# Five places of a two-layer decoder kernel reordered: the dilated fetch, the last pair result, the first gate, the weight differences and the last square of the final norm

## The chip, the core and the metric

The kernel runs on one core of one Trainium2 chip. The metric is the device time of one execution in microseconds (us), lower is better. Engines are called by the profile's names: PE (matmuls and transposes), PEld (its weight loads), DVE and ACT (elementwise work, ACT also the activation functions), POOL, and SP, which here only issues DMA transfers.

## The reference

The reference is a decoder trunk of two layers over 1024 tokens of width 1024, in 32-bit floating point. Cut to what matters, one layer is:

```
h    = rmsnorm(x, norm1[l]);  proj = h @ w_in[l]        # q, k, v of two mixers, and two gates
o_a  = dilated_mixture(qa, ka, va)                      # 3 groups of 4 heads: (window, dilation) = (128, 1), (512, 4), (2048, 16)
o_b  = stick_breaking_attention(qb, kb, vb)             # 4 heads: beta * product of (1 - beta) over later keys
x    = x + (sigmoid(gates_a) * (o_a @ w_br[:A]) + sigmoid(gates_b) * (o_b @ w_br[A:])) @ w_o[l]
h2   = rmsnorm(x, norm2[l]);  a, v = split(h2 @ w_up[l])
x    = x + (gelu(conv3(a)) * v) @ w_down[l]
```

Behind both layers stands one more `rmsnorm(x, norm_f)`, whose result is the output. A `rmsnorm` divides each token by the root of the mean of its squares over the 1024 features.

## The kernel before

**Products.** All activations lie with features on the partitions and tokens along the rows, in two halves of 512 tokens (`n` = 0 and 1). A 32-bit operand is split into a rounded high part and the rest: `split` (L138) does it with a cast on ACT (L141) and a subtraction on DVE (L148), and a product is then three matmuls, high by high, high by low and low by high (L1014 to L1016). Names ending in `h` or `hi` are high parts, names ending in `l` or `lo` low ones.

**Pairs.** The input projection is made pair by pair: `pair` (L1114) loads two blocks of 128 columns of `w_in` (tile `in_a`, L1128, two transfers of 512 KB) and makes both blocks for both token halves with seven products in place of eight. For that it forms sums and differences of weight quarters on DVE (L1142, L1145, L1148, L1149), splits them (`piece`, tiles `w_hi` and `w_lo`) and adds the products up afterwards. The last of the four results is copied out of the accumulation bank by L1198 (tile `last`) and handed to `put(1, 1, ...)`. For keys and queries of the dilated groups `put` is that of `pair_kq` (L1202 to L1215): it splits the result into high and low part (`in_parts`, L597 on ACT and L598 on DVE; tiles `kq_h` and, in place, `last`) and issues two stores to a scratch tensor `tk` in memory (L1211, SP).

**Attention between the products.** A generator, called `Dense` in the code, hands out the pair products step by step; items of attention work are placed between them, so that PE always has a product to do while ACT and DVE work for attention. `dense.at(k, f)` runs `f` after k more such steps. A stick-breaking item computes scores `z` (L644, L645), two sigmoids on ACT (`beta`, L711; `stay`, L712), a scan along the keys on DVE (L731 for the first stretch of keys, L733 for the others), a multiplication of `beta` by the scanned `stay` on DVE (L738), transposes on PE (`sb_t`, L746), a split into `sbh` and `sbl`, and the product with the values. A near item takes the first of the three dilated groups; its statistics leave by way of `st_r` (L842, L843). A far item takes the two groups of dilation 4 and 16: `fetch_kq` (L866 to L874) loads its keys and queries from `tk` with three transfers (L872: 384 KB; L874: two of 128 KB) into one of two tiles `t_kq`, used in turn, then `score` (L644, L645) reads the tile, and transposed probabilities `t` are split into `p1h` (ACT) and `p1l` (DVE) and multiplied by the values (L931, L933; accumulation tile `o`). `fold` (L659 on ACT, L660 on DVE) brings a finished `o` out. There are 16 far items in each layer; `fetch_v` (L878) loads their values.

**Gates and branches.** When the last pairs run, the stored gates come back (`gin`, L1358) and `gate_on` (L1360 to L1364) applies the sigmoid with two instructions per tile. In front of the first of them ACT loads another table of functions (`ACT_TABLE_LOAD`). At the same time `in_two` splits the stick-breaking output into `oh_b` and `ol_b`.

**The end.** `leave` (L1866) makes the final norm. `norm_add` (L470) squares a block of features (`sq`, ACT, L477) and adds it to `ACC` (`nrm`, DVE, L479). `factor` (L1872) sums `ACC` over the partitions with matmuls against a column of ones (L1877), takes the root (L1878) and the reciprocal (L1879). `turned` (L1881) transposes the result back to token rows (`y_t`, L1884), and `out_part` scales it and stores it (L1891, L1893, L1895).

**What sets the order.** PE runs in the order in which the code was recorded. The order on ACT, DVE, SP and POOL comes from a scheduler that simulates the program and works by priorities; `tc.high_priority(offset=AHEAD)` lifts instructions above others, and `tc.add_manual_dep(a, b, NO_SYNC)` puts instruction `a` somewhere behind `b` in an engine's order, without a semaphore. The dictionary `LAST` holds names of instructions to stand behind: `LAST["act"]` and `LAST["dve"]` are the two halves of the latest split of attention probabilities (`parts`, L647), `LAST["pair"]` the latest pair result. Each engine starts its instructions in its own fixed order, and an instruction that waits for a semaphore holds up those behind it. On SP that holds for the issue of transfers.

In the names below, numbers behind an underscore tell buffers of one name apart; `x2` at the end of a row of an order means two such instructions in a row.

Of the kernel before, what the change touches and what calls it, by code (L numbers as in the profile page):

```python
# [16 lines left out]
P = 128  # L17
# [39 lines left out]
def f32(ap):  # L57
    return ap.bitcast(F32)
# [3 lines left out]
def trunk_kernel(ctx, tc, x, norm1, w_in, b_gate, w_br, w_o, norm2, w_up, conv_w, conv_b, w_down, norm_f, out, depth=None, probe=None):  # L62
# [404 lines left out]

    ACC = [None, None]

    def norm_add(n, e, first=False, sub=slice(0, HF)):  # L470
# [6 lines left out]
        act.activation(sq, xc(n, e, sub), AF.Square)  # L477
        if not first:
            dve.tensor_tensor(acc, acc, sq, ALU.add)  # L479

# [114 lines left out]
    def in_parts(c, scale, hi, lo, x):  # L595
        if c:
            one = act.mul(hi, x, scale)  # L597
            two = dve.scalar_tensor_tensor(lo, x, scale, f32(hi), ALU.mult, ALU.subtract)  # L598
        else:
            one = act.copy(hi, x)  # L600
            two = dve.tensor_tensor(lo, x, f32(hi), ALU.subtract)
        return one.ins.name, two.ins.name

    def kq_half(c, w, n):
        o = bank("ps", "kq_ps"[c:])
        yield from product(o, [(w[k], h_part(n, k)) for k in range(KD)])
        hi, lo = small("kq_h", F32R), small("kq_l", F32R)
        LAST["head"] = in_parts(c, SCALE, hi, lo, o)
        LAST["pair"] = LAST["head"][0]
        keep_kq(c, n, 0, hi, lo)  # L610
        yield
# [82 lines left out]
    def stick_item(dense, u, qp):  # L694
# [29 lines left out]
        def scans(most):  # L724

            while SCANS and most:
                most -= 1
                _, bt, sv, c0, c1, L = SCANS.pop(0)
                rev = sv[:, c0:c1][:, ::-1]
                if c1 == L:  # L730
                    one = dve.tensor_tensor_scan(rev, rev, over[:, HF - (c1 - c0) : HF][:, ::-1], 1.0, ALU.mult, ALU.max)  # L731
                else:
                    one = dve.tensor_tensor_scan(rev, rev, zero[:, 0:1].to_broadcast([P, c1 - c0]), sv[:, c1 : c1 + 1], ALU.mult, ALU.add)  # L733
                if "dve" in LAST:
                    tc.add_manual_dep(one.ins, LAST["dve"], NO_SYNC, reason="in turn")
                k0, k1 = max(0, c0 - 1), c1 - 1
                with tc.high_priority(offset=AHEAD):
                    dve.tensor_tensor(bt[:, k0:k1], bt[:, k0:k1], sv[:, k0 + 1 : k1 + 1], ALU.mult)  # L738

        def turn(kb):  # L740
            while any(x[0] is shared and x[4] > kb * P for x in SCANS):
# [124 lines left out]
    def fetch_kq(i):  # L866

        if i < 2:
            t = R["kq", i] = sb.tile([P, 2, 3, 256], F32R, tag="xa", bufs=4, name="t_kq")
            pool.memset(f32(t[64:128, :, 2, :]), 0.0)  # L870
        t, there = R["kq", i % 2], tk[i // 8][i // 4 % 2, :, i % 4]
        nc.sync.dma_start(f32(t[0:64]), there[:, :, 1:4, :])  # L872
        for g in range(2):
            nc.sync.dma_start(f32(t[64:128, g, 0:2, :]), there[:, g, 0:3:2, :])  # L874

    def fetch_v(i):
        t = R["v", i] = R["slots"][:, i % 4]
# [236 lines left out]
    def pair(dense, l, offs, tiled, put):  # L1114
# [33 lines left out]
        yields(after(dve.tensor_tensor(a21, a22, a11, ALU.subtract)))  # L1148
        yields(after(dve.tensor_tensor(a11, a12, a11, ALU.subtract)))  # L1149
# [52 lines left out]
    def pair_kq(dense, l, g, pr):  # L1202
        off = 256 * g + P * pr

        def put(c, n, x, room=None):
            hi = room.bitcast(F32R) if room is not None else small("kq_h", F32R)
            hv, lv, xv = (t.rearrange("p (r j) -> p r j", r=4) for t in (hi, x.bitcast(F32R), x))
            in_parts(c, -SCALE, hv, lv, xv)
# [66 lines left out]
    def mixer(l, pending):  # L1275
# [84 lines left out]
        def gate_on(i):  # L1360
            if i < len(todo):
                n, e = todo[i]
                for ab in range(2):
                    act.activation(gts[i][:, ab, :], gts[i][:, ab, :], AF.Sigmoid, bias=bg[:, 0, ab * KD + e : ab * KD + e + 1])  # L1364

        def gate_in(i):
            gate_load(i)
# [498 lines left out]
    def leave(rest):  # L1866
# [5 lines left out]
        def factor(n, cs, tag="t"):  # L1872

            tot = bank(tag, "nrm_t")
            a, b = 4 * n + cs[0], 4 * n + cs[-1] + 1
            for c in cs:
                pe.matmul(tot[:, c : c + 1], ACC[n][:, c * P : (c + 1) * P], ones, start=True, stop=True, skip_group_check=True)  # L1877
# [27 lines left out]
        def features():  # L1905
            for e in range(4):
                yield from rest(5, e)
                norm_add(1, 4 + e, e == 0)
                gain_in(1, 4 + e)

        def tokens(sub):
            for e in range(4):
                for _ in rest(6, e, sub):
                    pass
                norm_add(1, e, False, sub)
                gain_in(1, e, sub)
                yield

# [17 lines left out]
        factor(1, (2, 3), "ps")  # L1936
        some += [turned(1, 2, 0, "ps"), turned(1, 3, 0, "s")]
        for t in some:
            out_part(*t)
# [211 lines left out]
```

## Time and profile before

| | |
|---|---|
| time, median of 3 runs | 2620.95 us (2620.76 to 2621.39) |
| time of the profiled execution | 2621.54 us |
| its span in the profile | 2619.8 us |
| granted TensorE clock | 1.000 |
| PE busy | 2606.3 us, 99% of the span |
| DVE busy | 2089.1 us, 80% |
| ACT busy | 1358.8 us, 52% |
| POOL busy | 100.4 us, 4% |
| moved by DMA | 468.22 MB, 179 GB/s |

The profiled execution took 0.59 us more than the median of the runs. Rows of the profile begin with a start time in us from the start of the span; then comes a duration, the engine, the line of the kernel, the operation, output and inputs, and, where the engine was idle before it, how long and what it waited for. Ends of matmuls are modelled: the profile gives a matmul of 512 columns some 0.39 us, while the next one may start 0.23 us after it. Layer 0 runs in about the first half of the span, layer 1 in the second; the same places come again some 1293 us later.

### The profile page before, as it was taken

The page shows a single profiled execution, that of the slowest core. Times are in us where ns is not written, and L with a number is a line of the kernel's source. Part 1 is how long each engine was busy: PE and PEld are TensorE (multiplying, and loading weights), DVE is VectorE, ACT ScalarE, POOL GpSimd, SP SyncE. Part 2 cuts the span into 40 slices and gives each one's busy share as a digit, 9 for nine tenths or more (in the row PEclk, how much of TensorE's full clock was granted, in tenths as well). Part 3 has the DMA queues.
Part 4 walks back from the last instruction along what each step waited for, and adds up shares of the span by engine and source line. Part 5 has one row for each costly group of instructions (what it writes and reads, how often), then busy time and mean ns, then how long its engine had stood idle before and what let it go on. Part 6 is the DMA issues. An engine that isn't in the chain of part 4 may idle for free.

```text
span 2619.8 us, 36195 instructions
## 1 busy us (share of the span) xinstructions
PE 2606.3 (99%) x12732; PEld 2185.4 (83%) x12732; DVE 2089.1 (80%) x3485; ACT 1358.8 (52%) x2533; POOL 100.4 (4%) x135
## 2 busy tenths in 40 slices
PE   9999999999999999999999999999999999999999
PEld 8888888888888888888888888888888888888887
DVE  8877777795988888897677778777869888889965
ACT  6555666574554555422445555666645555544225
POOL 3000000030000000000000000000300000000000
PEclk9999999999999999999999999999999999999999
DMA  7434578873344444688344436787633344446962
GB/s 255 152 117 135 163 202 219 212 245 93 93 145 154 143 169 137 240 325 311 145 150 141 129 124 187 198 224 212 209 97 116 129 156 150 147 167 257 347 240 112
DMA packets 400418, 468.22 MB, mean 179 GB/s; under 512 B 24309, under 2 KB 315501, under 8 KB 398445
## 3 DMA queue, kind: packets, MB, share of 16 engines
q1 hardware_dynamic: 400220, 465.90, 55.1%
q8 instruction: 101, 1.65, 0.3%
q14 instruction: 81, 0.66, 0.1%
q10 hardware_dynamic: 16, 0.00, 0.0%
HBM read 303.23 MB, written 162.59 MB: 178 GB/s over the span
## 4 chain that ended last, share of the span: by engine, by line
PE 94%; DVE 2%; ACT 2%; DMA 1%; issue 1%; SPq 0%; POOL 0%; DVEq 0%; ACTq 0%; POOLq 0%
PE u_a L1014 6%; PE u_a L1016 6%; PE u_a L1015 6%; PE d_ps L1763 5%; PE d_ps L1764 5%; PE d_ps L1765 5%; PE i_a L1014 5%; PE i_a L1016 4%; PE i_a L1015 4%; PE u_c L1014 3%; PE u_c L1016 3%; PE u_c L1015 3%; PE i_c L1014 2%; PE i_c L1016 2%; PE i_c L1015 2%; PE o_ps L182 2%
## 5 line engine op out<-in xcount | busy, mean ns | idle before, releaser
L141 ACT CAST w_hi<-up_a 128x512 fp32r<-128x512 f32 x280 | 174.0, 622 | 277.1 <-DVE up_a L1617 120.6
L148 DVE TENSOR_TENSOR w_lo<-up_a,w_hi 128x512 fp32r<-128x512 f32 x280 | 189.6, 689 | 83.4 <-ACT w_hi L141 83.4
L141 ACT CAST w_hi<-in_a 128x512 fp32r<-128x512 f32 x252 | 156.1, 622 | 163.4 <-PE i_c L1015 38.3
L148 DVE TENSOR_TENSOR w_lo<-in_a,w_hi 128x512 fp32r<-128x512 f32 x252 | 173.0, 688 | 74.9 <-ACT w_hi L141 65.8
L1771 DVE TENSOR_TENSOR x<-x,d_ps 128x512 f32<-128x512 f32 (+1 forms) x228 | 153.8, 676 | 64.9 <-PE d_ps L1765 61.5
L1763 PE MATMUL d_ps<-gd_in,w_hi 128*128 128x512 f32 (+1 forms) x340 | 130.1, 383 | 0.0
L1764 PE MATMUL d_ps<-gd_in,w_hi 128*128 128x512 f32 (+1 forms) x340 | 129.9, 382 | 0.0
L1765 PE MATMUL d_ps<-gd_in,w_lo 128*128 128x512 f32 (+1 forms) x340 | 129.9, 382 | 0.0
L1014 PE MATMUL u_a<-t_hi,w_hi 128*128 128x512 f32 x320 | 124.6, 389 | 0.0
L1016 PE MATMUL u_a<-t_hi,w_lo 128*128 128x512 f32 x320 | 124.6, 389 | 0.0
L1015 PE MATMUL u_a<-t_lo,w_hi 128*128 128x512 f32 x320 | 124.6, 389 | 0.0
L1016 PE MATMUL u_a<-hh,w_lo 128*128 128x512 f32 x320 | 124.6, 389 | 0.0
L1014 PE MATMUL u_a<-hh,w_hi 128*128 128x512 f32 x320 | 124.6, 389 | 0.0
L1015 PE MATMUL u_a<-hl,w_hi 128*128 128x512 f32 x320 | 124.6, 389 | 0.0
L1014 PE MATMUL i_a<-hh,w_hi 128*128 128x512 f32 x288 | 119.2, 414 | 0.0
L1014 PE MATMUL i_a<-t_hi,w_hi 128*128 128x512 f32 x288 | 118.4, 411 | 0.0
L1763 PE MATMUL d_ps<-gd_in,wd 128*128 128x512 f32 (+1 forms) x292 | 114.0, 390 | 0.0
L1016 PE MATMUL i_a<-hh,w_lo 128*128 128x512 f32 x288 | 113.2, 393 | 0.0
L1016 PE MATMUL i_a<-t_hi,w_lo 128*128 128x512 f32 x288 | 113.1, 393 | 0.0
L1015 PE MATMUL i_a<-t_lo,w_hi 128*128 128x512 f32 x288 | 113.0, 392 | 0.0
L1765 PE MATMUL d_ps<-gd_in,wd 128*128 128x512 f32 (+1 forms) x292 | 112.9, 387 | 0.0
L1764 PE MATMUL d_ps<-gd_in,wd 128*128 128x512 f32 (+1 forms) x292 | 112.9, 387 | 0.0
(379 smaller groups left out, 7839.6 us busy)
## 6 DMA issues: line engine op xcount, KB each, us to landing
gd<-g SPq DMA_DIRECT2D x154, 512.0 KB, 3.3
gd_in<-gd SPq DMA_DIRECT2D x154, 512.0 KB, 6.2
up_a<-in_w_up_dram SPq DMA_DIRECT2D x80, 512.0 KB, 5.3
in_a<-in_w_in_dram SPq DMA_DIRECT2D x72, 512.0 KB, 5.4
wd_raw<-in_w_down_dram SPq DMA_DIRECT2D x22, 1024.0 KB, 11.2
gin<-gs SPq DMA_DIRECT2D x32, 512.0 KB, 4.3
w_raw<-in_w_o_dram SPq DMA_DIRECT2D x64, 256.0 KB, 2.9
gs<-u SPq DMA_DIRECT2D x48, 256.0 KB, 4.0
```

The lines of the kernel that those rows point to most:

```text
L141: one = act.copy(hi, src)
L148: two = dve.tensor_tensor(lo, src, f32(hi), ALU.subtract)
L182: pe.matmul(o, lh, rh, start=(first and i == 0), stop=False, skip_group_check=share)
L1014: pe.matmul(o, w[0][:, c], rh, start=(first and i == 0), stop=False, skip_group_check=True)
L1015: pe.matmul(o, w[0][:, c], rl, start=False, stop=False, skip_group_check=True)
L1016: pe.matmul(o, w[1][:, c], rh, start=False, stop=(last and i == 3), skip_group_check=True)
L1763: pe.matmul(o[:, sub], wh[:, c], gh[:, sub], start=(i == 0 and k in (0, 4, 5)), stop=False, skip_group_check=True)
L1764: pe.matmul(o[:, sub], wh[:, c], gl[:, sub], start=False, stop=False, skip_group_check=True)
L1765: pe.matmul(o[:, sub], wl[:, c], gh[:, sub], start=False, stop=(i == m - 1), skip_group_check=True)
L1771: dve.tensor_tensor(x, x, o[:, sub], ALU.add)
```

## The change

There are five edits.

1. Dilated fetch: the three transfers of `fetch_kq` are issued at high priority.
2. Last pair result: for the pairs of dilated keys and queries, the split and the two stores of the last result run two steps later, and the split is put behind the latest split of probabilities on both engines.
3. First gate: the two sigmoids of the first gate tile are put behind the latest cast of probabilities on ACT.
4. Weight differences: the two differences that used to be L1148 and L1149 (now both L1152) are put behind the latest multiplication of `beta` by `stay` on DVE.
5. Last square: the last block of squares is not added to `ACC` by DVE. `factor` sums it with two matmuls of its own, into the same columns, and only the first matmul of the group opens the bank.

```
--- before.py
+++ after.py
@@ -467,7 +467,7 @@
 
     ACC = [None, None]
 
-    def norm_add(n, e, first=False, sub=slice(0, HF)):
+    def norm_add(n, e, first=False, sub=slice(0, HF), last=False):
 
         if first:
             ACC[n] = sb.tile([P, HF], F32, tag="ql", bufs=2, name="nrm")
@@ -475,6 +475,8 @@
         acc = acc[:, sub]
         sq = acc if first else small("sq")[:, sub]
         act.activation(sq, xc(n, e, sub), AF.Square)
+        if last:
+            return sq
         if not first:
             dve.tensor_tensor(acc, acc, sq, ALU.add)
 
@@ -599,13 +601,13 @@
         else:
             one = act.copy(hi, x)
             two = dve.tensor_tensor(lo, x, f32(hi), ALU.subtract)
-        return one.ins.name, two.ins.name
+        return one.ins, two.ins
 
     def kq_half(c, w, n):
         o = bank("ps", "kq_ps"[c:])
         yield from product(o, [(w[k], h_part(n, k)) for k in range(KD)])
         hi, lo = small("kq_h", F32R), small("kq_l", F32R)
-        LAST["head"] = in_parts(c, SCALE, hi, lo, o)
+        LAST["head"] = [x.name for x in in_parts(c, SCALE, hi, lo, o)]
         LAST["pair"] = LAST["head"][0]
         keep_kq(c, n, 0, hi, lo)
         yield
@@ -735,7 +737,7 @@
                     tc.add_manual_dep(one.ins, LAST["dve"], NO_SYNC, reason="in turn")
                 k0, k1 = max(0, c0 - 1), c1 - 1
                 with tc.high_priority(offset=AHEAD):
-                    dve.tensor_tensor(bt[:, k0:k1], bt[:, k0:k1], sv[:, k0 + 1 : k1 + 1], ALU.mult)
+                    LAST["mult"] = dve.tensor_tensor(bt[:, k0:k1], bt[:, k0:k1], sv[:, k0 + 1 : k1 + 1], ALU.mult).ins.name
 
         def turn(kb):
             while any(x[0] is shared and x[4] > kb * P for x in SCANS):
@@ -869,9 +871,10 @@
             t = R["kq", i] = sb.tile([P, 2, 3, 256], F32R, tag="xa", bufs=4, name="t_kq")
             pool.memset(f32(t[64:128, :, 2, :]), 0.0)
         t, there = R["kq", i % 2], tk[i // 8][i // 4 % 2, :, i % 4]
-        nc.sync.dma_start(f32(t[0:64]), there[:, :, 1:4, :])
-        for g in range(2):
-            nc.sync.dma_start(f32(t[64:128, g, 0:2, :]), there[:, g, 0:3:2, :])
+        with tc.high_priority(offset=AHEAD):
+            nc.sync.dma_start(f32(t[0:64]), there[:, :, 1:4, :])
+            for g in range(2):
+                nc.sync.dma_start(f32(t[64:128, g, 0:2, :]), there[:, g, 0:3:2, :])
 
     def fetch_v(i):
         t = R["v", i] = R["slots"][:, i % 4]
@@ -1145,8 +1148,11 @@
         yields(after(dve.tensor_tensor(a11, a21, a11, ALU.subtract)))
         w6 = piece(a11, None, [LAST["pair"]] * 2)
         yield
-        yields(after(dve.tensor_tensor(a21, a22, a11, ALU.subtract)))
-        yields(after(dve.tensor_tensor(a11, a12, a11, ALU.subtract)))
+        for dst, src in ((a21, a22), (a11, a12)):
+            one = after(dve.tensor_tensor(dst, src, a11, ALU.subtract))
+            if "mult" in LAST:
+                tc.add_manual_dep(one.ins, LAST["mult"], NO_SYNC, reason="behind")
+            yields(one)
         yield
         w3 = piece(a11, "waits")
         u = sb.tile([P, T], F32, tag="wr", bufs=NRAW, name="u")
@@ -1203,9 +1209,18 @@
         off = 256 * g + P * pr
 
         def put(c, n, x, room=None):
+            if (c, n) == (1, 1):
+                dense.at(2, lambda: store(c, n, x, room))
+            else:
+                store(c, n, x, room)
+
+        def store(c, n, x, room):
             hi = room.bitcast(F32R) if room is not None else small("kq_h", F32R)
             hv, lv, xv = (t.rearrange("p (r j) -> p r j", r=4) for t in (hi, x.bitcast(F32R), x))
-            in_parts(c, -SCALE, hv, lv, xv)
+            names = in_parts(c, -SCALE, hv, lv, xv)
+            if (c, n) == (1, 1) and "act" in LAST:
+                for one, there in zip(names, (LAST["act"], LAST["dve"])):
+                    tc.add_manual_dep(one, there, NO_SYNC, reason="in turn")
             for src, kind in ((hv, 1 + c), (lv, 3 * c)):
                 there = tk[pr][:, :, :, g - 1, kind, n * P : (n + 1) * P]
                 nc.sync.dma_start(there.rearrange("s p r j -> (s p) r j"), f32(src))
@@ -1361,7 +1376,9 @@
             if i < len(todo):
                 n, e = todo[i]
                 for ab in range(2):
-                    act.activation(gts[i][:, ab, :], gts[i][:, ab, :], AF.Sigmoid, bias=bg[:, 0, ab * KD + e : ab * KD + e + 1])
+                    one = act.activation(gts[i][:, ab, :], gts[i][:, ab, :], AF.Sigmoid, bias=bg[:, 0, ab * KD + e : ab * KD + e + 1])
+                    if i == 0:
+                        tc.add_manual_dep(one.ins, LAST["act"], NO_SYNC, reason="behind")
 
         def gate_in(i):
             gate_load(i)
@@ -1869,12 +1886,14 @@
         fs = sb.tile([P, 8], F32, tag="ss", bufs=2, name="fs")
         ys = [sb.tile([P, 4, D], F32, tag=tag, name="y") for tag in ("hh0", "hl0")]
 
-        def factor(n, cs, tag="t"):
+        def factor(n, cs, tag="t", more=None):
 
             tot = bank(tag, "nrm_t")
             a, b = 4 * n + cs[0], 4 * n + cs[-1] + 1
             for c in cs:
-                pe.matmul(tot[:, c : c + 1], ACC[n][:, c * P : (c + 1) * P], ones, start=True, stop=True, skip_group_check=True)
+                pe.matmul(tot[:, c : c + 1], ACC[n][:, c * P : (c + 1) * P], ones, start=(c == cs[0] or more is None), stop=more is None, skip_group_check=True)
+            for i, c in enumerate(cs if more is not None else ()):
+                pe.matmul(tot[:, c : c + 1], more[:, i * P : (i + 1) * P], ones, start=False, stop=True, skip_group_check=True)
             act.activation(ss[:, a:b], tot[:, cs[0] : cs[-1] + 1], AF.Sqrt, bias=eps[:, 0:1], scale=1.0 / D)
             dve.reciprocal(fs[:, a:b], ss[:, a:b])
 
@@ -1908,11 +1927,13 @@
                 norm_add(1, 4 + e, e == 0)
                 gain_in(1, 4 + e)
 
+        left = []
+
         def tokens(sub):
             for e in range(4):
                 for _ in rest(6, e, sub):
                     pass
-                norm_add(1, e, False, sub)
+                left.append(norm_add(1, e, False, sub, last=e == 3 and sub.stop == HF))
                 gain_in(1, e, sub)
                 yield
 
@@ -1933,7 +1954,7 @@
         for d2 in range(2):
             out_part(*turned(1, 1, d2))
         some = [turned(1, c, 1, "t") for c in (2, 3)]
-        factor(1, (2, 3), "ps")
+        factor(1, (2, 3), "ps", left[-1])
         some += [turned(1, 2, 0, "ps"), turned(1, 3, 0, "s")]
         for t in some:
             out_part(*t)
```

PE's order differs only by the two matmuls of edit 5. On the other engines the scheduler's order moves at several places; three of them follow. Lines below the edits have new numbers in the changed kernel.

The first is SP, late in the dilated part of layer 0, where the first far items are fetched: `t_kq_4607` is the tile of item 1, `tk1_92<-kq_h` and `tk1_92<-last` are the stores of a last pair result. SP before:

```order
L872 DMA t_kq_4365<-tk0_91 64x2x768
L874 DMA t_kq_4365<-tk0_91 64x2x256
L1211 DMA tk1_92<-in_a_3979 512x1x128
L1211 DMA tk1_92<-u_4271 512x1x128
L874 DMA t_kq_4365<-tk0_91 64x2x256
L872 DMA t_kq_4607<-tk0_91 64x2x768
L1211 DMA tk1_92<-kq_h_4575 512x1x128
L1211 DMA tk1_92<-last_4573 512x1x128
L843 DMA dn1_107<-st0_r_4587 32x128
L1128 DMA in_a_4590<-in_w_in_dram 128x8x128 x2
L874 DMA t_kq_4607<-tk0_91 64x2x256 x2
```

SP of the changed kernel, at the same place:

```order
L875 DMA t_kq_4365<-tk0_91 64x2x768
L877 DMA t_kq_4365<-tk0_91 64x2x256 x2
L1226 DMA tk1_92<-in_a_3974 512x1x128
L1226 DMA tk1_92<-u_4271 512x1x128
L875 DMA t_kq_4607<-tk0_91 64x2x768
L877 DMA t_kq_4607<-tk0_91 64x2x256 x2
L845 DMA dn1_107<-st0_r_4582 32x128
L1131 DMA in_a_4585<-in_w_in_dram 128x8x128 x2
L1226 DMA tk1_92<-kq_h_4602 512x1x128
L1226 DMA tk1_92<-last_4573 512x1x128
```

The three transfers of each fetch now stand together, ahead of the two stores of the last pair result and of the two weight loads.

The second is ACT at the same time, around the last pair result of that place; `kq_h` is its high part, `p1h_4619` the first probabilities of far item 0. ACT before:

```order
L1198 COPY last_4573<-i_a_4274 128x512
L141 CAST w_hi_4593<-in_a_4264 128x512
L597 ACTIVATE kq_h_4575<-last_4573 128x512
L659 COPY fold_4582<-o0_4539 64x512
L842 COPY st0_r_4587<-st0_t_4585 32x128
L141 CAST p1h_4619<-t1_4615 128x384
```

ACT of the changed kernel:

```order
L1204 COPY last_4573<-i_a_4274 128x512
L661 COPY fold_4577<-o0_4539 64x512
L844 COPY st0_r_4582<-st0_t_4580 32x128
L141 CAST w_hi_4588<-in_a_4264 128x512
L599 ACTIVATE kq_h_4602<-last_4573 128x512
L141 CAST p1h_4619<-t1_4615 128x384
```

The copies of `fold` and `st0_r` moved ahead of `w_hi` and `kq_h`; `kq_h` still stands ahead of `p1h`. On DVE the row `on<-o,fold` (L660, now L662) moved in the same way ahead of `w_lo` and `last`, and `last` still stands ahead of `p1l`.

The third is ACT where the first gate of layer 0 is opened; `gin_5872` is its tile. ACT before:

```order
L141 CAST oh_b_5953<-ob_in_5870 128x512
L1364 ACT_TABLE_LOAD
L1364 ACTIVATE gin_5872<-gin_5872,bg_82 128x512
L141 CAST p1h_5841<-t1_5837 128x384
L1364 ACTIVATE gin_5872<-gin_5872,bg_82 128x512
L141 CAST oh_b_5953<-ob_in_5870 128x512 x3
```

ACT of the changed kernel:

```order
L141 CAST oh_b_5953<-ob_in_5870 128x512 x2
L141 CAST p1h_5841<-t1_5837 128x384
L1379 ACT_TABLE_LOAD
L1379 ACTIVATE gin_5872<-gin_5872,bg_82 128x512 x2
L141 CAST oh_b_5953<-ob_in_5870 128x512 x2
```

The cast `p1h_5841` now stands ahead of the table load and of both sigmoids, behind one more `oh_b`. On DVE `p1l_5842` moved with it: ahead of the addition `u<-u,i_c` (L1175, now L1181), behind one more `ol_b`.

More of the change, by code (lines that the diff above doesn't have):

```diff
@@ L871, in fetch_kq @@
         t, there = R["kq", i % 2], tk[i // 8][i // 4 % 2, :, i % 4]
-        nc.sync.dma_start(f32(t[0:64]), there[:, :, 1:4, :])
-        for g in range(2):
-            nc.sync.dma_start(f32(t[64:128, g, 0:2, :]), there[:, g, 0:3:2, :])
+        with tc.high_priority(offset=AHEAD):
+            nc.sync.dma_start(f32(t[0:64]), there[:, :, 1:4, :])
+            for g in range(2):
+                nc.sync.dma_start(f32(t[64:128, g, 0:2, :]), there[:, g, 0:3:2, :])
     def fetch_v(i):
@@ L1147, in pair @@
         yield
-        yields(after(dve.tensor_tensor(a21, a22, a11, ALU.subtract)))
-        yields(after(dve.tensor_tensor(a11, a12, a11, ALU.subtract)))
+        for dst, src in ((a21, a22), (a11, a12)):
+            one = after(dve.tensor_tensor(dst, src, a11, ALU.subtract))
+            if "mult" in LAST:
+                tc.add_manual_dep(one.ins, LAST["mult"], NO_SYNC, reason="behind")
+            yields(one)
         yield
@@ L1876, in factor @@
             for c in cs:
-                pe.matmul(tot[:, c : c + 1], ACC[n][:, c * P : (c + 1) * P], ones, start=True, stop=True, skip_group_check=True)
+                pe.matmul(tot[:, c : c + 1], ACC[n][:, c * P : (c + 1) * P], ones, start=(c == cs[0] or more is None), stop=more is None, skip_group_check=True)
+            for i, c in enumerate(cs if more is not None else ()):
+                pe.matmul(tot[:, c : c + 1], more[:, i * P : (i + 1) * P], ones, start=False, stop=True, skip_group_check=True)
             act.activation(ss[:, a:b], tot[:, cs[0] : cs[-1] + 1], AF.Sqrt, bias=eps[:, 0:1], scale=1.0 / D)
@@ L1909, in features @@
                 gain_in(1, 4 + e)
+        left = []
         def tokens(sub):
```

30 lines of the change are left out of this document (21 added, 9 removed).

## The prediction

> **What bounds the kernel now.** I read the busy shares first, then the chain that ended last, then what PE waited for. The first two are on the page of the profile:
>
> ```profile
> PE 2606.3 (99%) x12732; PEld 2185.4 (83%) x12732; DVE 2089.1 (80%) x3485; ACT 1358.8 (52%) x2533; POOL 100.4 (4%) x135
> PE 94%; DVE 2%; ACT 2%; DMA 1%; issue 1%; SPq 0%; POOL 0%; DVEq 0%; ACTq 0%; POOLq 0%
> ```
>
> PE is busy for 2606.3 of 2619.8 us and carries 94% of the chain. PE's own work doesn't change here but for two small matmuls at the end, so the change can win only what PE waits, 13.5 us in all. The view of waits, for PE alone, says where most of that is; columns are the sum in us, the times, and the longest:
>
> ```profile
> PE z L644 <- DMA t_kq<-tk: 1.8, 2, 1.5
> ...
> PE o L931 <- DVE p1l L148: 1.3, 4, 0.5
> PE sb_t L746 <- DVE beta L738: 0.9, 2, 0.5
> ```
>
> These rows are what the first four edits aim at: 1.8 + 1.3 + 0.9 = 4.0 us. The counts 2, 4 and 2 fit one set of places in each of the two layers. The true loss is larger, since a wait is counted from the modelled end of the matmul before. I therefore take start-to-start distances and subtract what the same matmul takes when nothing is awaited: 0.23 us for 512 columns, 0.12 for 256, 0.11 for 128, as the unwaited starts below show.
>
> **Edit 4, weight differences.** DVE at the place in layer 0, then PE:
>
> ```profile
> 208.36 1.21 DVE L731 TENSOR_TENSOR_SCAN stay<-stay,over 128x512 f32<-128x512 f32 x1
> 209.49 0.66 DVE L1148 TENSOR_TENSOR in_a<-in_a 128x512 f32<-128x512 f32 x1
> 210.07 0.77 DVE L738 TENSOR_TENSOR beta<-beta,stay 128x512 f32<-128x512 f32 x1
> ```
> ```profile
> 210.19 0.28 PE L746 MATMUL sb_t<-ident,beta 128*128 128x128 f32 x1
> 210.90 0.44 PE L746 MATMUL sb_t<-ident,beta 128*128 128x128 f32 x2 [0.44 <-DVE beta L738]
> ```
>
> PE loses 0.71 - 0.11 = 0.60 us. The difference L1148 stands between the scan and the multiplication that reads it. In the new order the multiplication follows the scan at once. It can't start at 209.49 as L1148 did, since it needs the scan's last result at 209.57. Elsewhere a multiplication directly behind its scan begins 0.14 after the scan's end:
>
> ```profile
> 141.13 1.22 DVE L731 TENSOR_TENSOR_SCAN stay<-stay,over 128x512 f32<-128x512 f32 x1 [0.77 <-ACT stay L712]
> 142.49 0.69 DVE L738 TENSOR_TENSOR beta<-beta,stay 128x512 f32<-128x512 f32 x1
> ```
>
> So it starts at about 209.70 in place of 210.07: 0.37 us per layer, **0.74** for two. Bounds: 0 (something else is late) and 2 x 0.60 = 1.20.
>
> **Edit 2, last pair result.** ACT, DVE and PE before the first far product of layer 0:
>
> ```profile
> 419.82 0.62 ACT L141 CAST w_hi<-in_a 128x512 fp32r<-128x512 f32 x1 [0.44 <-DVE in_a L1149]
> ...
> 421.77 0.47 ACT L141 CAST p1h<-t 128x384 fp32r<-128x384 f32 x1
> ```
> ```profile
> 422.51 0.56 DVE L148 TENSOR_TENSOR p1l<-t,p1h 128x384 fp32r<-128x384 f32 x1
> ```
> ```profile
> 422.29 0.39 PE L931 MATMUL o<-p1h,slots 128*128 128x256 f32 x1
> 423.12 0.38 PE L931 MATMUL o<-p1l,slots 128*128 128x256 f32 x1 [0.45 <-DVE p1l L148]
> 423.35 0.22 PE L933 MATMUL o<-p1h,slots 128*128 128x128 f32 x1
> ```
>
> PE loses 0.83 - 0.12 = 0.71 us, and 0.11 more at the restart (423.35 - 423.12 is 0.23, not 0.12): 0.82 per layer. The edit is meant to take `kq_h` and `last` out of the way of `p1h` and `p1l`, but in the new order both still stand ahead of them. What moves is `fold`, `st_r` and, on DVE, `on`, from behind `w_hi` and `kq_h` to ahead of them. ACT stood idle for 0.44 us before `w_hi`, and `fold` and `st_r`, whose inputs PE has finished by then, fill that gap. So `p1h` starts 0.5 to 0.6 earlier, and DVE, which no longer has `on` to do just before `p1l` (0.71 by its neighbours' distances), follows: `p1l` near 421.95 in place of 422.51. Of 0.82 that saves about 0.55 per layer, **1.10** for two, and some 0.25 per layer stays. Bounds 0 and 1.64. The stores of this result are issued later; who waits for that is below.
>
> **Edit 1, dilated fetch.** The chain of waits in layer 1, and PE in layer 0:
>
> ```profile
> 1718.08 7.64 DMA t_kq<-tk
> ...
> 1725.86 0.30 PE z L644
> ```
> ```profile
> 444.79 0.27 PE L645 MATMUL z<-t_kq 128*128 128x128 f32 x1
> 445.40 0.33 PE L644 MATMUL z<-t_kq 128*128 128x128 f32 x1 [0.34 <-DMA t_kq<-tk]
> ```
>
> In layer 1 the last third of item 1's fetch is issued at 1718.08, behind the loads and stores that the order of SP shows, lands after 7.64 us, and PE waits 1.50 by the waits, 1.67 from start to start (the matmul before it counts 0.39 where 0.23 is its due). In layer 0 the same place is late by under 0.1, and item 4's fetch holds PE for 0.61 - 0.11 = 0.50. In the new order all three thirds of item 1 stand ahead of the weight loads and of the late stores, so the last is issued some 5 us earlier in layer 1; even at 7.64 us it then lands 3 us before PE asks. Item 4's stand ahead of two stores that wait for ACT and DVE, and are out by 436.4 and not 438.8. Gain 0.50 + 0.08 + 1.67 = **2.25**, bounds 0 and 2.25.
>
> **Edit 3, first gate.** ACT, DVE and PE of layer 0:
>
> ```profile
> 528.81 0.64 ACT L141 CAST oh_b<-ob_in 128x512 fp32r<-128x512 f32 x1
> 529.47 1.28 ACT L1364 ACT_TABLE_LOAD   x1
> 530.77 0.73 ACT L1364 ACTIVATE gin<-gin,bg 128x512 f32<-128x512 f32 x1
> 531.40 0.46 ACT L141 CAST p1h<-t 128x384 fp32r<-128x384 f32 x1
> ```
> ```profile
> 531.29 0.40 PE L1016 MATMUL i_a<-t_hi,w_lo 128*128 128x512 f32 x1
> 531.91 0.39 PE L931 MATMUL o<-p1h,slots 128*128 128x256 f32 x1 [0.22 <-ACT p1h L141]
> 532.50 0.38 PE L931 MATMUL o<-p1l,slots 128*128 128x256 f32 x1 [0.21 <-DVE p1l L148]
> ```
>
> PE loses 0.62 - 0.23 = 0.39 for `p1h`, 0.59 - 0.12 = 0.47 for `p1l` and, as in the pair, some 0.10 at the restart: 0.96 per layer. The table load (1.28) and one sigmoid (0.73) now come behind `p1h`; one more `oh_b` (0.52 from start to start) comes ahead of it. So `p1h` starts near 529.9 and `p1l` near 530.9, done by 531.45, where PE asks at 531.52 and 531.64. The slack is only some 0.15, but the wait should be gone: **1.92**, bounds 0 and 1.92. The `fold` behind the sigmoids keeps its own time, since ACT does the same work up to there.
>
> **Edit 5, last square.** PE near the end, and DVE:
>
> ```profile
> 2612.65 0.61 PE L1877 MATMUL nrm_t<-ones,nrm 128*128 128x1 f32 x4
> 2613.12 1.07 PE L1884 MATMUL y_t<-ident,x 128*128 128x128 f32 x8
> ```
> ```profile
> 2612.18 0.41 DVE L479 TENSOR_TENSOR nrm<-nrm,sq 128x256 f32<-128x256 f32 x1
> ```
>
> The two matmuls show as four records, 0.47 us from 2612.65 to the next start. The DVE addition that goes ended at 2612.59, and PE came from a row of sixteen transposes, so taking it out frees nothing that shows. Two more matmuls of the same shape put the root, the reciprocal and the last stores back by 0.47; I take 0.44 (four records of 0.11). So this edit **costs 0.44**; bounds -0.1 (if the transposes had been held up) and 0.5. [...]
>
> **The sum.** 0.74 + 1.10 + 2.25 + 1.92 - 0.44 = 5.57 us saved. Against the profiled execution's 2621.54 that is 2615.97; it stood 0.59 above the median, so the median comes out at **2615.4 us**, 0.21% faster. A measurement of this kernel tells about 0.2% (5.24 us, the line at 2615.7) from no change, and the forecast stands almost on that line. If all bounds fell well, it would be 2620.95 - 1.20 - 1.64 - 2.25 - 1.92 - 0.1 = 2613.8; if all fell ill, 2621.5.
>
> **Rivals.**
>
> *The fetch only moves its wait.* Item 3's tile is free when PE has read item 1. Its three transfers go out from 431.87, the last near 433.2, and PE asks at 439.50:
>
> ```profile
> 431.87 0.59 SPq L874 DMA_DIRECT2D t_kq<-tk  x1
> ```
> ```profile
> 439.50 0.22 PE L644 MATMUL z<-t_kq 128*128 128x128 f32 x1
> ```
>
> That leaves 6.3 us. If item 1's 7.64 us came from the fetch's own small rows and not from the loads ahead of it, item 3 lands 1.3 us late, in both layers: 2.6 lost, 2618.0. For it: item 4's fetch, too, took about 7 us (issued from 437.6, read at 445.40). Against it: in both cases other transfers stood directly ahead of the late part, weight loads in the one and two stores in the other, and item 3's own last third goes out at 435.6 now, two us later than in the new order, and is not waited for. Chance 0.17.
>
> *The pair edit doesn't do what it says*, because `kq_h` and `last` keep their place: its 1.10 falls away, or most of edit 3 does, where the slack is 0.15. 2616.5 to 2617.4. Chance 0.13.
>
> *Weights late behind multiplications.* At 91 to 98 us the differences now stand behind a second scan and two multiplications (1.21 + 0.77 by the rows above). The low part that PE needs next was made at 97.17; now one `sbl` stands ahead of it, and it ends near 98.6. DVE before, and PE, which needs it at 99.03:
>
> ```profile
> 97.17 0.69 DVE L148 TENSOR_TENSOR w_lo<-in_a,w_hi 128x512 fp32r<-128x512 f32 x1
> ```
> ```profile
> 99.03 0.40 PE L1016 MATMUL i_c<-hh,w_lo 128*128 128x512 f32 x1
> ```
>
> With 0.4 of slack, a shift longer by the whole 1.98 costs 1.6 per layer: 2618.6. [...] Chance 0.07.
>
> *Slower: SP's queue is held up.* The stores of the last pair result now stand behind item 7's fetch, which waits for PE to read item 5 (that is from about 453, since the items' reads of `t_kq` follow each other by 5 to 7 us here). Item 8's fetch reads what they store, and can't be issued before PE has read item 6, at about 459.7; PE asks for it at:
>
> ```profile
> 471.92 0.22 PE L644 MATMUL z<-t_kq 128*128 128x128 f32 x1
> ```
>
> I expect the stores at 455 to 456. From 459.7 there are 12.2 us to the read, of which a fetch needs up to 9.5 (7.64 from its last issue, and 1.9 for three issues of 0.6). Beyond that, each us by which the stores land later stops PE for one us, in each layer. It decides the sign only when PE loses 5.4 us per layer: 2626.2 and up. Chance 0.04.
>
> **How the numbers follow.** Forecast 0.59, with its own range 2613.8 to 2616.4: 0.48 of it faster by over 0.2%, 0.11 within. The first three rivals (0.37) are within 0.2%, but for 0.01 of the fetch rival: with item 3 late by only a tenth the time stays under the line. Faster 0.49, same 0.47, slower 0.04. The range 2613.8 to 2619.5 leaves out the slower rival, some 0.05 below and 0.07 above.
>
> **What would show it.** Right: PE's waits for `t_kq`, for `beta` and for `p1h` gone, that for `p1l` smaller; `nrm_t` with eight records and the root 0.4 us further from the end of the last `d_ps`. Wrong: a wait of PE at 439, 99 or 472 us and at the same places 1293 us on, `p1l` of the pair still 0.8 late, or a last part that is no longer.

## The result, and the profile after

The changed kernel takes 2616.52 us, median of 20 runs (2615.33 to 2618.31); the kernel before took 2621.36 us in 20 runs beside it (2620.14 to 2622.95). The ratio is 0.9982, with a 95% interval of 0.9975 to 0.9988: 4.84 us less. The forecast was 5.57 us less (0.9979), inside that interval; the time lies in the range 2613.8 to 2619.5. It is 0.18% less, and the forecast was 0.21%: the two lie on either side of the line at 0.2%, about equally near to it. The forecast gave these two sides 0.49 and 0.47, so the side on which the time fell says nothing for or against its mechanism.

The profiled execution of the changed kernel took 2618.04 us, with a span of 2616.1; it is one of the slowest of the 20. Its page has these two lines on the busy shares and on the chain that ended last:

```profile
PE 2606.0 (100%) x12736; PEld 2185.2 (84%) x12736; DVE 2089.5 (80%) x3484; ACT 1357.6 (52%) x2533; POOL 102.2 (4%) x135
PE 96%; DVE 1%; DMA 1%; ACT 1%; issue 1%; SPq 0%; POOL 0%; DVEq 0%; ACTq 0%
```

PE's work is the same (four records more), its share of the chain rose from 94 to 96%, those of DVE and ACT fell. What PE waits for, in the same view as before:

```profile
PE warm L2062 <- POOL ident masks.py:199: 1.8, 1, 1.8
PE z L646 <- ACT stay L714: 0.5, 2, 0.2
PE o_ps L183 <- POOL hl L1399: 0.5, 1, 0.5
PE nrm_t L536 <- DVE nrm L481: 0.4, 2, 0.2
...
PE o_ps L182 <- DVE x L1286: 0.2, 1, 0.2
```

The rows for `t_kq`, `beta`, `p1l` and `p1h` are gone; together they were 4.4 us. Two rows for `o_ps` are new: PE waits at the first output products behind the gates. The view has one more new row, 0.2 us for `v_ps` at 9.5 us, at the start of the kernel.

PE runs the same instructions in the same order in both kernels, up to the last norm. So the start of one and the same matmul can be compared between two traces, and a step in the difference is what a place gained or lost. The table has the step at each place (median difference behind it minus the median ahead of it), for this execution and for a second one of the same kernel (run `again`, below). Layer 0 / layer 1, us:

| place | forecast | changed kernel | again |
|---|---|---|---|
| weight differences, 211 / 1504 | -0.74 in all | -0.45 / -0.46 | -0.44 / -0.47 |
| last pair result, 423 / 1716 | -1.10 | -0.46 / -0.45 | -0.46 / -0.45 |
| fetch, 431 to 445 / 1726 | -2.25 | -0.65 / -1.78 | -0.66 / -1.79 |
| first gate, 532 / 1827 | -1.92 | -0.96 / -0.97 | -0.96 / -0.97 |
| last norm, to its root | +0.44 | +0.32 | +0.32 |
| first output products, 590 / 1891 | 0 | +0.75 / +0.49 | +0.03 / 0.00 |
| start of the kernel, before 60 | 0 | +0.96 | -0.02 |

The first five rows come to -5.9 us in both and barely differ between the two. The last two rows are where these two executions differ; beside them `again` gains 0.28 us near 1970, at a norm where the profiled executions of the kernel before and of the changed kernel both wait. All steps are taken against one profiled execution of the kernel before, and its own chance waits are in them: for the fetch this matters, as the single edits show below.

### The profile page after: what moved, and what is told of

Its sections match the earlier page's. It is cut to its first block, busy times and chain, and to the rows that moved or that the text cites. A ratio compares the mean times of both kernels' runs of the same rounds, so it can differ in the third digit from the quotient of the medians.

```text
span 2616.1 us, 36210 instructions
## 1 busy us (share of the span) xinstructions
PE 2606.0 (100%) x12736; PEld 2185.2 (84%) x12736; DVE 2089.5 (80%) x3484; ACT 1357.6 (52%) x2533; POOL 102.2 (4%) x135
## 4 chain that ended last, share of the span: by engine, by line
PE 96%; DVE 1%; DMA 1%; ACT 1%; issue 1%; SPq 0%; POOL 0%; DVEq 0%; ACTq 0%
PE u_a L1019 6%; PE u_a L1018 6%; PE u_a L1017 6%; PE d_ps L1780 5%; PE d_ps L1781 5%; PE d_ps L1782 5%; PE i_a L1017 5%; PE i_a L1019 5%; PE i_a L1018 5%; PE u_c L1017 3%; PE u_c L1019 3%; PE u_c L1018 3%; PE i_c L1017 3%; PE i_c L1019 3%; PE i_c L1018 3%; PE o_ps L183 2%
## 5 line engine op out<-in xcount | busy, mean ns | idle before, releaser
L1780 PE MATMUL d_ps<-gd_in,wd 128*128 128x512 f32 (+1 forms) x292 | 113.9, 390 | 0.0
L1018 PE MATMUL i_a<-hl,w_hi 128*128 128x512 f32 x288 | 112.8, 392 | 0.0
L1782 PE MATMUL d_ps<-gd_in,wd 128*128 128x512 f32 (+1 forms) x292 | 112.8, 386 | 0.0
```

What stands on the lines that cost most here:

```text
L1018: pe.matmul(o, w[0][:, c], rl, start=False, stop=False, skip_group_check=True)
L1780: pe.matmul(o[:, sub], wh[:, c], gh[:, sub], start=(i == 0 and k in (0, 4, 5)), stop=False, skip_group_check=True)
L1782: pe.matmul(o[:, sub], wl[:, c], gh[:, sub], start=False, stop=(i == m - 1), skip_group_check=True)
```

## The experiments

**Once more, and the gate.** The new waits at `o_ps` could be the price of edit 3, or the chance of one execution. Four kernels were measured side by side. Run `again` is the changed kernel unaltered:

> The changed kernel once more, unaltered. Theory A (the stage of the gates is paced by its own chain of gate loads, ACT, DVE and POOL, so that part of what PE gains in front of it is given back at the first output products): PE waits again at the first o_ps products of layer 0 or layer 1, 0.3 to 1.0 us in all. Rival B (those waits were the jitter of one execution): no wait of PE above 0.2 us at o_ps. By both: 4 to 5.5 us under the kernel before, and no wait for t_kq, beta or p1h.

Measured: 2616.09 us (2615.55 to 2618.29), ratio 0.9979 (0.9971 to 0.9988). Its waits of PE, whole:

```profile
PE warm L2062 <- POOL ident masks.py:199: 1.8, 1, 1.8
PE z L646 <- ACT stay L714: 0.5, 2, 0.2
PE x_t L1997 <- DVE xsq L2015: 0.3, 1, 0.3
PE gb L2078 <- DVE g L2075: 0.3, 1, 0.3
PE v_ps L184 <- DVE hl L148: 0.2, 1, 0.2
PE nrm_t L536 <- DVE nrm L481: 0.2, 1, 0.2
```

No `o_ps`. A price that is always paid is ruled out.

`gate_only` is the kernel before with edit 3 alone:

```diff
+                    one = act.activation(gts[i][:, ab, :], gts[i][:, ab, :], AF.Sigmoid, ...)
+                    if i == 0:
+                        tc.add_manual_dep(one.ins, LAST["act"], NO_SYNC, reason="behind")
```

> Only edit 3 (first gate). A: PE's waits for p1h and p1l at 532 and 1827 go (1.9 us by start-to-start distances), and PE waits 0.3 to 1.0 us for hl or x at o_ps behind the gates, so that 0.9 to 1.6 us are left of it. B: the whole 1.9 us come out, and o_ps does not wait more than in the kernel before.

Measured: 2620.51 us (ratio 0.9995, 0.9986 to 1.0004), 1.0 less than the kernel before beside it, with no change inside the interval. In the trace the place gives -0.96 and -0.97, and 0.21 comes back at `o_ps` of layer 1. PE at the first gate:

```profile
531.51 0.28 PE L931 MATMUL o<-p1h,slots 128*128 128x256 f32 x1
531.63 0.28 PE L931 MATMUL o<-p1l,slots 128*128 128x256 f32 x1
```

`no_gate` is the changed kernel without those lines:

> The changed kernel without edit 3. The waits for p1h and p1l at the first gate are back (1.9 us). A: o_ps waits less than in the changed kernel, so the loss against the changed kernel is only 0.9 to 1.6 us. B: 1.9 us slower than the changed kernel.

Measured: 2617.86 us (ratio 0.9986, 0.9977 to 0.9995), 1.77 above `again` beside it; the steps at 532 and 1827 are +0.01 and 0.00, so the waits are back in full. At its own place edit 3 is worth 1.9 us. The times agree when it is taken out (1.77); when it is put in alone they show 1.0, and where the rest of that goes is not shown, but for the 0.21 above. Of the waits at `o_ps` this can be said: nine profiled executions here have edit 3, and in 5 of their 18 passes PE lost 0.2 to 0.75 us there, 0.3 us per execution on the mean; four kernels without it, and their 8 passes, show 0.00. (A pass is one layer of one execution.) That would fit a PE that now arrives earlier than the chain of the gates sometimes does; with 5 of 18 against 0 of 8 it is not shown.

**The last square.** `no_square` is the changed kernel without edit 5:

```diff
-        factor(1, (2, 3), "ps", left[-1])
+        factor(1, (2, 3), "ps")
```

with DVE's addition and the one-step `factor` of the kernel before.

> The changed kernel without edit 5 (last square). If the four extra records of 128x1 are paid in full, as the prediction says: 0.35 to 0.45 us faster than the changed kernel, the root 0.4 us nearer to the end of the last products. [...] If taking the addition off DVE is worth something: slower than the changed kernel.

Measured: 2616.22 us (ratio 0.9979, 0.9970 to 0.9988), not to be told from `again`. The traces tell: PE at the end of the changed kernel, and of `no_square`:

```profile
2606.88 0.28 PE L1782 MATMUL d_ps<-gd_in,w_lo 128*128 128x256 f32 x1
2607.00 1.91 PE L1903 MATMUL y_t<-ident,x 128*128 128x128 f32 x16
2608.74 0.50 PE L1894 MATMUL nrm_t<-ones,nrm 128*128 128x1 f32 x4
2609.11 0.58 PE L1896 MATMUL nrm_t<-ones,sq 128*128 128x1 f32 x4
2609.55 1.07 PE L1903 MATMUL y_t<-ident,x 128*128 128x128 f32 x8
```
```profile
2605.57 0.28 PE L1780 MATMUL d_ps<-gd_in,w_lo 128*128 128x256 f32 x1
2605.69 1.91 PE L1899 MATMUL y_t<-ident,x 128*128 128x128 f32 x16
2607.46 0.61 PE L1892 MATMUL nrm_t<-ones,nrm 128*128 128x1 f32 x4
2607.93 1.07 PE L1899 MATMUL y_t<-ident,x 128*128 128x128 f32 x8
```

From the last `d_ps` to the transposes behind the sums it is 2.67 us with edit 5 and 2.36 without: 0.31. The root starts 2.86 and 2.54 us after that `d_ps`, the last scaling ends 4.83 and 4.52 after it. Edit 5, where it stands, costs 0.32 us.

**Where edit 5 could pay.** In `factor_early` the sums are called eight transposes earlier, right behind the last square:

```diff
-        some = [turned(1, c, 1, "t") for c in (2, 3)]
         factor(1, (2, 3), "ps", left[-1])
+        some = [turned(1, c, 1, "t") for c in (2, 3)]
```

> The changed kernel, with the sums of the last norm called eight transposes earlier. Theory (edit 5 costs its four records because sixteen transposes stood ahead and hid the DVE addition anyway; it can pay only if the sums stand right behind the last square): the root starts 2.2 to 2.4 us after the last d_ps matmul, in place of 2.86 in the changed kernel and 2.54 in the kernel before, and the last scaling ends 4.4 to 4.5 us after it, in place of 4.83 and 4.52. Rival (the last transposes set the end, not the root): the last scaling still ends 4.8 us after the last d_ps.

`early_dve` does the same without edit 5:

> The same earlier place of the sums, but without edit 5: the last square goes through DVE's addition, as in the kernel before. Theory: PE waits some 0.7 us for that addition, which stands behind a scaling on DVE; the root starts about 2.5 us after the last d_ps and the last scaling ends 4.7 to 4.9 us after it, so the early place alone is worth nothing and edit 5 is what makes it usable. Rival: the addition is not waited for, and the end is as in factor_early or better.

Measured: `factor_early` 2616.29 us (ratio 0.9980, 0.9972 to 0.9989); `early_dve` 2615.82 in its one run, which tells nothing at this size. PE and ACT of `factor_early`, then PE of `early_dve`:

```profile
2605.00 1.04 PE L1903 MATMUL y_t<-ident,x 128*128 128x128 f32 x8
2605.87 0.51 PE L1894 MATMUL nrm_t<-ones,nrm 128*128 128x1 f32 x4
2606.24 0.58 PE L1896 MATMUL nrm_t<-ones,sq 128*128 128x1 f32 x4
2606.68 1.95 PE L1903 MATMUL y_t<-ident,x 128*128 128x128 f32 x16
```
```profile
2607.09 0.25 ACT L1897 ACTIVATE ss<-nrm_t,eps 128x2 f32<-128x2 f32 x1
2607.79 1.27 ACT L1912 ACTIVATE y<-y_t,fs 128x512 f32<-128x512 f32 x2 [0.45 <-PE y_t L1903]
```
```profile
2606.75 0.61 PE L1892 MATMUL nrm_t<-ones,nrm 128*128 128x1 f32 x4 [0.74 <-DVE nrm L479]
2607.22 1.95 PE L1899 MATMUL y_t<-ident,x 128*128 128x128 f32 x16
```

The root of `factor_early` starts 2.21 us after the last `d_ps`, 0.65 sooner than in the changed kernel, but the scaling then waits for `y_t`: the last transposes set the end, and the last scaling ends 4.54 after, 0.29 sooner, which only pays back the four records. The theory was right on the root; for the end neither its 4.4 to 4.5 nor the rival's 4.8 came, though the rival named what sets it. In `early_dve`, without edit 5, PE stands 0.74 us for DVE's addition, the root starts 2.54 us after the last `d_ps`, and the last scaling ends 5.10 after it, later than the 4.7 to 4.9 expected. So edit 5 is what makes an early sum possible, and here an early sum is worth no more than edit 5 costs.

**The last pair result.** `pair_three` defers it by three steps:

```diff
-                dense.at(2, lambda: store(c, n, x, room))
+                dense.at(3, lambda: store(c, n, x, room))
```

> The changed kernel with the last pair result put off by three steps in place of two, which puts its split behind the first probabilities on ACT and DVE. If what is left of PE's wait for p1l at 423 and 1715 (0.23 us from start to start, 0.1 above that at the restart) is due to kq_h and last ahead of it: that wait goes, 0.2 to 0.35 us per layer. If it has another cause (the fold, the transposes): nothing changes there. In both cases the time is within 1 us of the changed kernel's.

Measured: 2616.62 us (ratio 0.9980, 0.9971 to 0.9989). First the chain of waits of the changed kernel in layer 1, then DVE and PE of `pair_three` in layer 0:

```profile
1713.74 0.60 DVE last L600
1714.34 0.48 DVE p1l L148
1714.82 0.04 issue
1714.87 0.39 PE o L934
```
```profile
421.27 1.01 DVE L148 TENSOR_TENSOR p1l<-t,p1h 128x384 fp32r<-128x384 f32 x2
```
```profile
422.12 0.28 PE L934 MATMUL o<-p1h,slots 128*128 128x256 f32 x1
422.24 0.28 PE L934 MATMUL o<-p1l,slots 128*128 128x256 f32 x1
```

In the changed kernel `last` still stands ahead of `p1l` and PE waits for it. With three steps it doesn't, PE goes from `p1h` to `p1l` in 0.12, and the place gives -0.80 / -0.79 in place of -0.46 / -0.45: the rest of the wait, 0.34 us per layer, was `kq_h` and `last`. In this one execution the first gate of layer 1 gave only -0.32, `o_ps` of layer 0 cost 0.65 and a place near 1618 another 0.5; whether the third step has to do with that is not shown. The median of eleven runs shows nothing of the 0.7 us.

`both` has the early sums and the three steps:

> The changed kernel with both of these, the earlier sums and the later pair result. If each does what its theory says, the sum is 0.4 + 0.5 us: 0.7 to 1.1 us under the changed kernel, which would make it the fastest; by the rivals, the changed kernel's time.

Measured: 2616.27 us (2615.28 to 2618.05; ratio 0.9979, 0.9970 to 0.9988). The steps are as in each alone (-0.80 / -0.79; last scaling 4.54 after the last `d_ps`), and `o_ps` took 0.55. At these places the trace gains 0.97 us over the changed kernel; the median of eleven runs, which spread over 2.8 us, is only 0.25 lower.

**The edits alone.** `fetch_only`, `pair_only` and `diff_only` are the kernel before with edit 1, 2 or 4, as in the change's diff.

> Only edit 1 (dilated fetch). Theory (the late third of item 1's fetch was slow because of the loads issued just ahead of it): it is issued ahead of the weight loads, lands in 4.5 to 5 us and not 7.6, and PE never waits for t_kq: 2.2 us by start-to-start distances. Rival (the fetch's own small rows make it slow, or the wait moves to item 3 or 4): 7 us to landing, or a new wait of PE for t_kq at another item.

Measured: 2619.09 us (ratio 0.9991, 0.9982 to 1.0001), 2.2 less, with no change just inside the interval. No wait for `t_kq`; the steps are -0.66 / -1.78. SP of `fetch_only` in layer 1:

```profile
1712.16 1.26 SPq L875 DMA_DIRECT2D t_kq<-tk  x2
1713.52 0.55 SPq L1212 DMA_DIRECT2D tk<-kq_h  x1
1714.32 0.54 SPq L1212 DMA_DIRECT2D tk<-last  x1
1714.96 0.67 SPq L843 DMA_DIRECT2D dn<-st_r  x1
1715.67 1.39 SPq L1129 DMA_DIRECT2D in_a<-in_w_in_dram  x2
```

The second of the two 128 KB transfers, issued ahead of the loads, lands 4.36 us after its issue. In the kernel before, with the loads just ahead, the row said 7.64 for the first of the two (both stood behind the loads there). `pair_only`, next, tells the loads from the stores.

> Only edit 2 (last pair result). PE's wait for p1l at 423 and 1716 falls from 0.7 to 0.1 to 0.35 us by start-to-start distances, 0.4 to 0.5 us per layer, since fold and st_r fill ACT's gap; the fetch waits of the kernel before remain, and may be longer, since the two stores now come later.

One run, 2621.04 us, of which 0.94 is the start of the kernel. The pair's place gives -0.46 / -0.45, as expected. But the waits for `t_kq`, expected to stay, are gone from the view of waits as well: -0.44 / -1.29 there. SP of `pair_only` in layer 1:

```profile
1714.44 0.32 SPq L843 DMA_DIRECT2D dn<-st_r  x1
1714.86 1.02 SPq L1128 DMA_DIRECT2D in_a<-in_w_in_dram  x2
1715.97 2.72 SPq L1220 DMA_DIRECT2D tk<-kq_h  x1
1718.74 1.25 SPq L1220 DMA_DIRECT2D tk<-last  x1
1720.05 1.88 SPq L874 DMA_DIRECT2D t_kq<-tk  x2
```

The two stores no longer hold the weight loads back: these go out at 1714.86 and not at 1716.43, and the first 128 KB transfer, although it is issued 2 us later than before and the stores now stand just ahead of it, lands after 4.58 us, in time but for half a us. So it was the loads just ahead, and not the stores, that made it slow.

> Only edit 4 (weight differences). PE's wait for beta at 211 and 1504 falls from 0.60 to 0.15 to 0.25 us by start-to-start distances, 0.37 to 0.45 us per layer. By the rival of the weights that come late behind multiplications, PE waits near 99 and 1392, up to 1.6 us; by the forecast it does not.

One run, 2620.79 us; -0.45 / -0.47 at the place. No wait near 99 or 1392; PE at the place of the rival:

```profile
99.14 0.39 PE L1015 MATMUL i_c<-hl,w_hi 128*128 128x512 f32 x1
99.38 0.40 PE L1016 MATMUL i_c<-hh,w_lo 128*128 128x512 f32 x1
```

**What the fetch loses without edits 1 and 2.** `gate_only` and `diff_only` have neither, so they are two more executions of the fetch as it was. In layer 1 they confirm it: the first 128 KB transfer lands after 7.59 and 7.44 us, and the steps against the kernel before are only -0.02 and -0.23. In layer 0 they do not: the wait for item 4, 0.50 in the forecast, is absent from both, and 0.2 us more is lost at item 1 in its place, so that the steps there are -0.30 and -0.35 with neither edit. PE of `gate_only` where the kernel before took 0.61 from one row to the next:

```profile
445.32 0.27 PE L645 MATMUL z<-t_kq 128*128 128x128 f32 x1
445.43 0.27 PE L644 MATMUL z<-t_kq 128*128 128x128 f32 x1
```

Against `fetch_only` the three executions lose 2.4, 2.1 and 1.9 us at the fetch, 2.1 on the mean. And of the -0.44 of `pair_only` in layer 0 at most some 0.15 is the doing of edit 2; its 1.3 us in layer 1 stand.

**Is edit 1 needed?** After `pair_only`, `no_fetch` is the changed kernel without edit 1:

> The changed kernel without edit 1 (dilated fetch). Theory after pair_only (either edit 1 or edit 2 takes the weight loads out of the way of item 1's late third, so their gains overlap): PE waits for t_kq by less than 0.5 us in all, and the time is within 0.6 us of the changed kernel's. Rival (pair_only was luck, edit 1 carries the 2.2 us): waits for t_kq of 1.5 us and more are back, and the time is some 2 us above the changed kernel's.

Measured: 2617.29 us (ratio 0.9985, 0.9976 to 0.9994). PE's waits for `t_kq` stay away but for these in layer 1, the first 0.30 late from start to start, the second 0.23:

```profile
1720.74 0.39 PE L1018 MATMUL i_c<-hh,w_lo 128*128 128x512 f32 x1
1721.27 0.30 PE L646 MATMUL z<-t_kq 128*128 128x128 f32 x1
1721.40 0.28 PE L647 MATMUL z<-t_kq 128*128 128x128 f32 x1
1721.74 0.33 PE L646 MATMUL z<-t_kq 128*128 128x128 f32 x1
```

The steps are -0.66 / -1.15 in place of -0.66 / -1.79. With edit 2 there, edit 1 is worth 0.6 us in this trace, a little more than the 0.5 of the theory and far from the 1.5 of the rival. The median stands 0.77 above the changed kernel's 2616.52 and 1.2 above that of `again`, measured at other times; with intervals of some 2 us on either side that decides nothing, and the trace carries the verdict.

## Why the prediction was right, point by point

- **PE is the bound, and only its waits can be won.** Right: every step of the table is a wait of PE that went or came, but for the last norm, where PE got more to do.
- **Weight differences, 0.74.** Mechanism right, size 0.91. The multiplication does start 0.13 us after its scan's end (L740 below, the forecast took 0.14), but it also took 0.69 us and not 0.77, and PE's wait left over is 0.15 per layer. DVE of the changed kernel:

```profile
209.35 1.21 DVE L733 TENSOR_TENSOR_SCAN stay<-stay,over 128x512 f32<-128x512 f32 x1
210.69 0.69 DVE L740 TENSOR_TENSOR beta<-beta,stay 128x512 f32<-128x512 f32 x1
```

- **Last pair result, 1.10.** Right that `kq_h` and `last` keep their place and leave a rest, and that `fold` and `st_r` fill ACT's gap (of the 0.44 us idle before `w_hi` nothing is left: `fold` starts at 420.04, `st_r` at 420.64, `w_hi` at 420.80); the gain is 0.91, the rest 0.34 per layer and not 0.25 (`pair_three`).
- **Fetch, 2.25.** Size 2.43 against the one execution that the forecast was read from, 2.1 on the mean of three. Right that the loads just ahead of it made it late in layer 1: 7.4 to 7.6 us to landing in three executions, 4.4 to 4.8 in three with edit 1 (`fetch_only`, the changed kernel, `again`). It was not one third, though: both 128 KB transfers stood behind the loads. Wrong in the attribution: the step put the whole gain down to edit 1 and put what edit 2's later stores do for the loads at nothing. Edit 2 alone brings 1.3 us in layer 1, since those two stores held the loads back. The gains overlap and can't be added; the sum came out because all of it stood under one edit. And the 0.50 for item 4 in layer 0 was a wait of that one execution, which two others of the same order lack; that this term agrees so well with the table, which is taken against the same execution, is no confirmation of it.
- **First gate, 1.92.** Right to 0.01, in every execution with the edit but one, where 0.65 us of the wait came back in layer 1 (`pair_three`); that would fit the slack of only 0.15 that the forecast named, and is not shown.
- **Last square, +0.44.** Right in sign, 0.32 in size: the four further records cost 0.08 each and not 0.11.
- **The sum.** 0.91 + 0.91 + 2.43 + 1.93 - 0.32 = 5.86 us by the places, against 5.57 forecast. The measured 4.84 (and 5.43 in `again`) is smaller. Some 0.3 of the difference is the fetch, which cost more in this one execution of the kernel before than on the mean of three, and waits at `o_ps` take 0.3 on the mean; what is left, 5.3, is within the intervals of both.
- **The rivals.** The fetch didn't move its wait to item 3, nor did the stores of the last pair result hold up item 8: there is no wait for `t_kq` in either profiled execution of the changed kernel, and the two stores were issued at 454.5 and 455.2, about as expected. The weights are not late at 99. That the pair edit doesn't do all it says was true for the rest that `pair_three` took out.

## What to carry to other kernels

Where one engine is the bound and its order is fixed, compare the start of the same instruction in two traces: a gain of 0.3 us shows there, where eleven timed runs, spread over 3 us, show nothing. But one trace is one execution: look into a second trace of the kernel before as well, or a chance wait is taken for a cost and its absence for a gain, as with item 4's fetch here. When two edits act on one queue, try each alone before giving a gain to either: here the stores of one held back the loads that delayed the other's fetch (in the kernel before the loads went out at 1716.43 us and the fetch's first 128 KB transfer landed after 7.64 us, in `pair_only` at 1714.86 and after 4.58). And work added to the bound engine was paid in full here (0.32 us for the four records of edit 5), except where it took a wait of that engine away at the very place where it was put (the 0.74 us of `early_dve`).

## What the runs showed of the hardware

- In layer 1, a 128 KB transfer of item 1's fetch issued just behind two loads of 512 KB landed after 7.44 to 7.64 us (the kernel before, `gate_only`, `diff_only`); one issued ahead of them 4.36 to 4.83 us after its issue (`fetch_only`, the changed kernel, `again`); and 4.58 when issued 5 us behind them (`pair_only`), 5.62 at 4 us behind (`no_fetch`).
- At three places an instruction that waited held up those behind it. PE stood 0.74 us before `nrm_t` in `early_dve`, with transposes behind it that `no_square` starts without a wait. ACT stood 0.44 us before `w_hi` at 419.82 in the kernel before, with `fold` behind it, whose input PE had made by 418.93. On SP the two loads went out at 1716.43 behind the two stores, and at 1714.86 when the stores stood behind them (`pair_only`).
- The same instructions differ between executions, mostly at two places: by up to 1 us in the first 60 us (`pair_only` 0.94, `factor_early` 0.66, `again` -0.02), and by up to 0.75 at the first output products. Single executions differ elsewhere too: by 0.8 us near 1618 (`no_gate`; 0.2 to 0.5 in `both`, `pair_only` and `pair_three`), and by 0.3 near 1970. At the edited places the steps repeat to within 0.15 us between kernels with the same edits there, but for the first gate of layer 1 in `pair_three`.
